# Input projections of both token mixers in seven block products, latents by way of DRAM, two dense down groups in one bank

## The chip, the cores and the metric

The kernel runs on one core of one Trainium2 chip. The metric is the device time of one execution in microseconds (us), taken as the median of several runs. Engines are named as in the profile: PE multiplies matrices, PEld loads its stationary operand, DVE (VectorE) and ACT (ScalarE) work element by element, POOL is GpSimd, and SP issues most transfers.

## What is computed

Two pre-norm residual layers on 1024 tokens of width 1024, then a final norm, all in float32. Each layer is a token mixer (latent attention and a gated recurrence side by side, fed by one input projection) and a channel mixer (a dense SwiGLU in layer 0, the top two of eight experts in layer 1).

```
for l in range(DEPTH):
    h = _rmsnorm(x, mix_norm[l])
    proj = h @ w_in[l]                          # 1024 x 1024 by 1024 x 2752
    c_q, c_kv, k_pe, hq, hf, hi, hg = jnp.split(proj, splits, axis=-1)
                                                # 384, 256, 64, then 4 x 512
    a = _mla(c_q, c_kv, k_pe, ...)              # latents normed, then w_q_b, w_kv_b, softmax
    r = _hgrn2(hq, hf, hi, hg, ...)             # 4 heads, chunkwise causal scan
    x = x + jnp.concatenate([a, r], axis=-1) @ w_out[l]
    h = _rmsnorm(x, ffn_norm[l])
    x = x + (_swiglu(h, ...) if l % 2 == 0 else _moe(h, ...))
return _rmsnorm(x, final_norm)
```

## The kernel before, in words

**Matmuls.** Every float32 operand of a matmul is split into a rounded high part (a copy on ACT, L162) and the rest (a subtraction on DVE, L163); `mm3` (L156 to L159) then multiplies high by high, high by low and low by high into the same bank. Most matmuls have 128 rows, 128 stationary columns and 512 moving columns.

**Input projection.** The norm of the eight token tiles (`norms`, `norm_tile`: square on ACT L184, power on POOL L181, multiplication on DVE L186) is followed tile by tile by eight transpositions on PE (L200) and a split of 128x1024 into the arena for split operands (FR). `Weights.parts` loads one block of 128 columns of w_in at a time (two raw buffers, SP) and splits it, again 128x1024. `proj` multiplies a block with the tokens: two halves of 512 tokens, eight steps in depth, three products, 48 matmuls. There are 22 blocks in a layer: three and two for the latents of queries and keys, one for the rotary key, then four for each of the four recurrence heads (forget gate, query, value, output gate). In layer 0 the first two blocks are done in pieces of 256 tokens, so that PE can start while later tiles arrive. Latents are squared on ACT from the bank, scaled on DVE (L354), summed on POOL (L353), and after the norm kept split in FR until attention uses them. Heads' values are evicted by ACT and DVE straight from the bank.

**Recurrence.** `hgrn` runs seven levels per head. A level copies a part of K (ACT, L455), multiplies four small products of 128 columns in two halves (PE, L487, eight matmuls), copies them under a mask into A (DVE, two operations, L494), and scales parts of Q and K by products of decays (DVE, four operations, L501). The next level's small products need those scaled parts. POOL makes the products of decays for the levels (L505). PE fills the time between levels with the projection of the next head, or, after the last head, with the first products of attention.

**Seven block products.** The dense gate and up projections already avoid one product in eight: operands are taken as 2 x 2 blocks, sums of blocks are formed, and seven products of blocks replace eight. `block_norms` makes the sums of the token operand (DVE and POOL) after the transpositions (L850), `block_sums` the sums of the weights (four POOL additions of 128x512, L879 to L884), `block_products` runs the seven products (L906, 12 matmuls of 512 columns each, 84 for a pair of column blocks) and combines them on eviction (four ACT copies, four DVE additions). For the first pair, `Gate.early` prepares three of the seven weight blocks, and their products run first over the first six token tiles (384 columns) and then over the last two (128 columns).

**Dense down.** Eleven groups of two blocks each; a group multiplies with all eight token tiles and DVE adds the bank to the residual x (`xt`). In the last group, a token tile's norm for layer 1 starts as soon as its two additions are done.

**Order.** A scheduler places the instructions; each engine then runs its own list in order, and waits where an operand isn't ready. Buffers are rings in two arenas, FF (float32) and FR (split operands).

## Time and profile before

| | |
|---|---|
| median of three runs | 3997.98 us (3994.89 to 4000.73) |
| profiled execution | 4001.75 us |
| its span, first to last instruction | 4000.0 us |
| mean granted clock of TensorE in it | 0.994 of full speed |
| PE busy | 3923.7 us (98%) |
| DVE, ACT, POOL busy | 2490.4, 1569.0, 353.5 us |

A row of a timeline gives start and duration in us, engine, line, operation, output and inputs with their shapes, the number of equal instructions in a row, and in brackets the idle time of the engine just before with what ended it. Rows of lines give a group's count, busy us and mean ns. Matmuls overlap each other, so the pace of PE is read from starts, not from durations.

The stages: layer 0's norm begins with the first transposition at 13 us, the small products of its recurrence heads start at 146, 210, 274 and 337 us, attention runs from about 371 to 531 us, then comes the output projection, the dense gate and up products from 622 to 1050 us, dense down to 1297 us; layer 1's mixer transposes its tokens from 1278 us on, and the experts run from 1933 us.

### The profile page before, as it was taken

The page shows a single profiled execution, that of the slowest core. Times are in us where ns is not written, and L with a number is a line of the kernel's source. Part 1 is how long each engine was busy: PE and PEld are TensorE (multiplying, and loading weights), DVE is VectorE, ACT ScalarE, POOL GpSimd, SP SyncE. Part 2 cuts the span into 40 slices and gives each one's busy share as a digit, 9 for nine tenths or more (in the row PEclk, how much of TensorE's full clock was granted, in tenths as well). Part 3 has the DMA queues.
Part 4 walks back from the last instruction along what each step waited for, and adds up shares of the span by engine and source line. Part 5 has one row for each costly group of instructions (what it writes and reads, how often), then busy time and mean ns, then how long its engine had stood idle before and what let it go on. Part 6 is the DMA issues. An engine that isn't in the chain of part 4 may idle for free. (4 is left out here: it accounts for less than half of the span.)

```text
span 4000.0 us, 62669 instructions
## 1 busy us (share of the span) xinstructions
PE 3923.7 (98%) x24870; PEld 3553.3 (89%) x24870; DVE 2490.4 (62%) x5624; ACT 1569.0 (39%) x2367; POOL 353.5 (9%) x406
## 2 busy tenths in 40 slices
PE   8999999999999999999899999999999999999998
PEld 7888887888788888888899999999999999999997
DVE  6455676554667454665655666776767765555665
ACT  3223434333312222442444334444444444444443
POOL 2100013233100101001200000000000000000011
PEclk9999999999999999999999999999999999999999
DMA  3111112222422111111665445455455555655674
GB/s 114 43 39 65 36 54 66 82 84 85 150 106 100 51 38 46 51 52 66 228 222 195 159 170 171 159 193 177 170 178 182 200 174 195 209 192 191 222 269 157
DMA packets 381228, 533.86 MB, mean 133 GB/s; under 512 B 15260, under 2 KB 317340, under 8 KB 380924
## 3 DMA queue, kind: packets, MB, share of 16 engines
q1 hardware_dynamic: 371142, 495.10, 37.1%
q0 software_dynamic: 7632, 26.95, 1.9%
q10 hardware_dynamic: 2150, 7.70, 0.5%
q8 instruction: 197, 3.23, 0.3%
q14 instruction: 107, 0.88, 0.1%
HBM read 478.82 MB, written 50.89 MB: 132 GB/s over the span
## 5 line engine op out<-in xcount | busy, mean ns | idle before, releaser
L157 PE MATMUL s<-fr_arena 128*128 128x256 f32 (+6 forms) x6816 | 2178.1, 320 | 11.1 <-ACT fr_arena L162 3.1
L158 PE MATMUL s<-fr_arena 128*128 128x256 f32 (+6 forms) x6816 | 2165.7, 318 | 0.0
L159 PE MATMUL s<-fr_arena 128*128 128x256 f32 (+6 forms) x6816 | 2162.7, 318 | 0.0
L157 PEld LDWEIGHTS s<-fr_arena 128*128 128x128 f32 x6816 | 1292.0, 190 | 94.0 <-ACT ff_arena L650 4.1
L159 PEld LDWEIGHTS s<-fr_arena 128*128 128x128 f32 x6816 | 1289.2, 189 | 75.2 <-DVE fr_arena L163 0.8
L158 PEld LDWEIGHTS s<-fr_arena 128*128 128x128 f32 x6816 | 1290.6, 189 | 71.5 <-DVE fr_arena L163 0.4
L1301 DVE TENSOR_TENSOR fr_arena<-ff_arena,fr_arena 128x256 fp32r<-128x256 f32 x2688 | 977.0, 418 | 552.6 <-ACT fr_arena L1298 548.2
L1298 ACT ACTIVATE fr_arena<-ff_arena 128x1024 fp32r<-128x1024 f32 x672 | 693.2, 1056 | 989.2 <-PE s L158 601.7
L162 ACT ACTIVATE fr_arena<-ff_arena 128x512 fp32r<-128x512 f32 (+7 forms) x598 | 354.8, 608 | 834.0 <-PE s L158 372.6
L163 DVE TENSOR_TENSOR fr_arena<-ff_arena,fr_arena 128x512 fp32r<-128x512 f32 (+8 forms) x598 | 419.6, 708 | 313.4 <-ACT fr_arena L162 244.3
L906 PE MATMUL s<-fr_arena 128*128 128x512 f32 (+2 forms) x1884 | 427.9, 389 | 0.7 <-ACT ff_arena L859 0.7
L906 PEld LDWEIGHTS s<-fr_arena 128*128 128x128 f32 x1884 | 350.3, 189 | 78.3 <-DVE ff_arena L924 4.1
L1408 DVE TENSOR_TENSOR ff_arena<-s,ff_arena 128x296 f32<-128x296 f32 (+3 forms) x416 | 176.2, 447 | 124.7 <-PE s L159 124.6
L1004 DVE TENSOR_TENSOR ff_arena<-s,ff_arena 128x512 f32<-128x512 f32 x176 | 119.1, 688 | 63.1 <-PE s L159 63.1
L162 ACT ACTIVATE fr_arena<-s 128x512 fp32r<-128x512 f32 (+7 forms) x182 | 109.8, 614 | 121.6 <-PE s L668 47.7
L1461 POOL DMA_DIRECT2D ff_arena<-xres x8 | 4.6, 576 | 1716.9 <-DMA ys<-ff_arena 1703.8
L163 DVE TENSOR_TENSOR fr_arena<-s,fr_arena 128x512 fp32r<-128x512 f32 (+7 forms) x182 | 126.6, 706 | 26.7 <-ACT fr_arena L162 24.6
L1362 DVE TENSOR_TENSOR ff_arena<-s,ff_arena 128x256 f32<-128x256 f32 (+4 forms) x224 | 95.8, 428 | 16.9 <-ACT ff_arena L1361 16.9
L1361 ACT ACTIVATE ff_arena<-s 128x256 f32<-128x256 f32 (+4 forms) x224 | 84.1, 376 | 23.0 <-PE s L159 23.0
L501 DVE TENSOR_TENSOR ff_arena<-ff_arena 128x256 f32<-128x256 f32 x224 | 84.5, 431 | 2.3 <-ACT ff_arena L455 1.5
L455 ACT ACTIVATE ff_arena<-ff_arena 128x256 f32<-128x256 f32 x112 | 42.8, 420 | 101.4 <-DVE ff_arena L501 42.5
L487 PEld LDWEIGHTS s<-ff_arena 128*128 128x128 f32 x448 | 55.4, 190 | 17.6 <-issue 14.2
(291 smaller groups left out, 1980.4 us busy)
## 6 DMA issues: line engine op xcount, KB each, us to landing
ff_arena<-in_moe_w_gate_dram SPq DMA_DIRECT2D x112, 1024.0 KB, 5.1
ff_arena<-in_moe_w_up_dram SPq DMA_DIRECT2D x112, 1024.0 KB, 7.5
ff_arena<-in_moe_w_down_dram SPq DMA_DIRECT2D x112, 1024.0 KB, 5.6
ff_arena<-in_w_in_dram SPq DMA_DIRECT2D x42, 512.0 KB, 4.0
ff_arena<-in_dense_w_gate_dram SPq DMA_DIRECT2D x11, 1024.0 KB, 5.8
ff_arena<-in_dense_w_up_dram SPq DMA_DIRECT2D x11, 1024.0 KB, 5.2
hidd<-ff_arena SPq DMA_DIRECT2D x44, 256.0 KB, 2.0
ff_arena<-hidd SPq DMA_DIRECT2D x11, 1024.0 KB, 6.6
```

The source lines that it names most:

```text
L157: nc.tensor.matmul(ps, lh, rh, start=first, stop=False)
L158: nc.tensor.matmul(ps, lh, rl, start=False, stop=False)
L159: nc.tensor.matmul(ps, ll, rh, start=False, stop=last)
L162: nc.scalar.activation(hi, src, AF.Copy)
L163: nc.vector.tensor_sub(lo, src, hi)
L501: nc.vector.tensor_mul(d, d, t)
L906: nc.tensor.matmul(ps, a[:, k, :], b[:, :, k, :], start=first and k + n == 0, stop=last and k == 3 and n == 2, skip_group_check=True)
L1004: nc.vector.tensor_add(xt[:, i, cs], ps, xt[:, i, cs])
L1298: nc.scalar.activation(hi, src, AF.Copy)
L1301: nc.vector.tensor_sub(lo[:, q:q + n], src[:, q:q + n], hi[:, q:q + n])
L1362: nc.vector.tensor_mul(s, ps[:, 1, 0:cap], s)
L1408: nc.vector.tensor_add(self.yT[:, k, :], ps[:, 0:cap], self.yT[:, k, :])
```

## The change

The mixers' input projections take the form of the dense gate's. `Weights` now holds eleven pairs of column blocks per layer: three for the latents with the rotary key, then two for each head (forget gate with query, value with output gate). `Weights.pair` forms the sums on POOL, splits seven weight blocks of 128x512 through a ring of twelve slots, runs the 84 matmuls, evicts by four ACT copies and four DVE additions into two float32 tiles of 1024, and loads the next pair into its only raw buffer. `early` prepares three blocks for the first pair as the gate does. The norm in front is `block_norms`; `norms`, `transpose_tile` and the pieces of 256 tokens are gone. What followed a bank before (sigmoids, squares, gains) now follows these tiles. The latents are normed in float32, written to a DRAM buffer `latd`, and read back and split by `attention`, whose first part runs before the last head's `hgrn` (`ahead`). The order of the seven products and of their evictions changes (for gate and up too). The last two dense down groups share one bank: 12 matmuls for each of the two banks of a token tile, 24 per tile, one DVE addition per bank in the place of two. Places in the arenas change throughout.

```
+            self.raw, self.s3 = view(FF, 4096, KD, 256), view(FF, 8192, 4, P)
+            self.wr = Ring(FR, 28672, 512, 12)
+            self.todo = [((0, 0, 256),), ((0, 256, 256),),
+                         ((0, 512, 192), (192, 672, 32), (224, 640, 32))]
+            self.todo += [((0, a, P), (P, b, P)) for a, b in hg]
...
+        def early(self):
+            self.load()
+            sums = block_sums(self.raw, self.s3)
+            self.ready = [block_parts(sums, self.wr) for _ in range(3)]
+            self.sums = iter([next(sums) for _ in range(4)])
+
+        def pair(self, d0, d1):
...
+            pa, pb = S2(), S2()
+            cs = [d.rearrange("p (q w t) -> p w q t", w=2, t=P)[:, w] for d in (d0, d1) for w in range(2)]
+            block_products(sums, self.wr, (pb[:, 0], pa[:, 0], pa[:, 1], pb[:, 1]), cs, ready)
+            if self.todo:
+                self.load()
...
+            for j in range((3, 2)[g]):
+                nc.sync.dma_start(latd[g * 3 + j], c32[g * 3 + j])
...
-        for u in range(2):
-            for b in range(2):
-                latent(b, u, first[b])
+        W.pair(c32[0], c32[1])
         if l == 0:
             setup_rope()
             setup_gates()
...
+        square(0)
+        square(1)
+        W.pair(c32[2], c32[3])
+        square(2)
+        square(3)
+        latent_rms(0)
...
         for h in range(H):
             f, K, Q, G, V = R["f"](T), R["k"](T), R["q"](T), R["g"](T), R["v"](NT, P)
-            ps = proj2(HC["f"] + h * P, rest if h == 0 else None)
-            nc.scalar.activation(f, ps, AF.Sigmoid)
-            nc.scalar.activation(K, ps, AF.Sigmoid, scale=-1.0)
+            W.pair(K, Q)
+            if h == 0:
+                rest()
+            nc.scalar.activation(f, K, AF.Sigmoid)
+            nc.scalar.activation(K, K, AF.Sigmoid, scale=-1.0)
...
+            if h == H - 1:
+                ahead()
             hgrn(h, f, K, Q, G, V, R)
...
+        for r, b, hl in raws[0:4]:
+            nc.sync.dma_start(r, latd[b])
         load_v(0)
         load_qk(0)
+        nc.sync.dma_start(tab, tabd)
+        for n, (r, b, hl) in enumerate(raws):
+            if n > 3:
+                nc.sync.dma_start(r, latd[b])
+            split(*hl, r)
+        yield
...
-    TN = ("B11", "B21", "T1", "T2", "B22", "T3", "T4")
+    TN = ("B21", "T1", "B11", "B22", "T2", "T4", "T3")
...
+        for i in range(NT):
+            for c in range(2):
+                cs = slice(c * 512, (c + 1) * 512)
+                ps = S1()
+                for b in range(4):
+                    mm3(ps, mv[i // 2][:, b, 0, i % 2], mv[i // 2][:, b, 1, i % 2], wv[:, b, 0, cs],
+                        wv[:, b, 1, cs], b == 0, b == 3)
+                nc.vector.tensor_add(xt[:, i, cs], ps, xt[:, i, cs])
+            post.tile(i)
```

Lines move: L162 and L163 become L174 and L175, the block transpositions L850 become L838, the block products L906 become L895 and their additions L906, the weights' sums L879 to L884 become L866 to L871, the recurrence's L494, L501 and L505 become L483, L490 and L494.

PE at the start of layer 0, before: transpositions of three tiles, then the projection in pieces of 256 tokens.

```order
L200 MATMUL s_126<-ident,ff_arena 128x128 x8
L200 MATMUL s_143<-ident,ff_arena 128x128 x8
L200 MATMUL s_161<-ident,ff_arena 128x128 x8
L157 MATMUL s_244<-fr_arena 128x256
L157 MATMUL s_295<-fr_arena 128x256
L158 MATMUL s_244<-fr_arena 128x256
L159 MATMUL s_244<-fr_arena 128x256
```

The same place after:

```order
L838 MATMUL s_126<-ident,ff_arena 128x128 x8
L838 MATMUL s_144<-ident,ff_arena 128x128 x8
L838 MATMUL s_184<-ident,ff_arena 128x128 x8
L838 MATMUL s_202<-ident,ff_arena 128x128 x8
L838 MATMUL s_231<-ident,ff_arena 128x128 x8
L838 MATMUL s_249<-ident,ff_arena 128x128 x8
L838 MATMUL s_273<-ident,ff_arena 128x128 x4
L838 MATMUL s_274<-ident,ff_arena 128x128 x4
L838 MATMUL s_287<-ident,ff_arena 128x128 x4
L838 MATMUL s_288<-ident,ff_arena 128x128 x4
L895 MATMUL s_312<-fr_arena 128x384 x24
L895 MATMUL s_313<-fr_arena 128x384 x12
```

The transpositions of all eight tiles now stand ahead of the first product, and that begins with 384 columns.

DVE in two levels of the recurrence, before (`s_2000`, `s_2014` and `s_2028` are the banks of the small products, masked copies L494, multiplications L501, a weight split L163):

```order
L494 COPY_PREDICATED ff_arena<-lmask,s_2000 128x4x16x4 x2
L501 TENSOR_TENSOR ff_arena<-ff_arena 128x4x16x4 x2
L501 TENSOR_TENSOR ff_arena<-ff_arena 128x4x4x16 x2
L494 COPY_PREDICATED ff_arena<-lmask,s_2014 128x4x8x8 x2
L501 TENSOR_TENSOR ff_arena<-ff_arena 128x4x8x8 x2
L501 TENSOR_TENSOR ff_arena<-ff_arena 128x4x2x32 x2
L163 TENSOR_TENSOR fr_arena<-ff_arena,fr_arena 128x1024
L494 COPY_PREDICATED ff_arena<-lmask,s_2028 128x4x4x16 x2
```

DVE in two levels after (masked copies L483, multiplications L490, L906 the eviction of a block product, L175 a weight split):

```order
L483 COPY_PREDICATED ff_arena<-lmask,s_2055 128x4x16x4 x2
L490 TENSOR_TENSOR ff_arena<-ff_arena 128x4x16x4 x2
L490 TENSOR_TENSOR ff_arena<-ff_arena 128x4x8x8 x2
L906 TENSOR_TENSOR ff_arena<-s_2201,ff_arena 128x4x128
L483 COPY_PREDICATED ff_arena<-lmask,s_2069 128x4x8x8 x2
L490 TENSOR_TENSOR ff_arena<-ff_arena 128x4x8x8 x2
L490 TENSOR_TENSOR ff_arena<-ff_arena 128x4x4x16 x2
L175 TENSOR_TENSOR fr_arena<-ff_arena,fr_arena 128x512
L483 COPY_PREDICATED ff_arena<-lmask,s_2083 128x4x4x16 x2
```

Before, a split of 1024 columns stood in every second level or so; now an operation of 512 columns stands in each.

POOL between two heads of layer 0, before (L505 the recurrence's products of decays, L181 a power for the read-out norm):

```order
L505 TENSOR_TENSOR ff_arena<-ff_arena 128x512
L505 TENSOR_TENSOR ff_arena<-ff_arena 128x256
L505 TENSOR_TENSOR ff_arena<-ff_arena 128x128
L505 TENSOR_TENSOR ff_arena<-ff_arena 128x64
L505 TENSOR_TENSOR ff_arena<-ff_arena 128x32
L505 TENSOR_TENSOR ff_arena<-ff_arena 128x16
L181 TENSOR_TENSOR rs_87<-rs_87,sm 128x4
L505 TENSOR_TENSOR ff_arena<-ff_arena 128x8
L181 TENSOR_TENSOR rs_87<-rs_87,sm 128x4
```

POOL between two heads after (L866 to L871 the sums of two pairs of weight blocks, L494 the products of decays):

```order
L866 TENSOR_TENSOR ff_arena<-ff_arena 128x512
L867 TENSOR_TENSOR ff_arena<-ff_arena 128x4x128
L870 TENSOR_TENSOR ff_arena<-ff_arena 128x4x128
L871 TENSOR_TENSOR ff_arena<-ff_arena 128x4x128
L866 TENSOR_TENSOR ff_arena<-ff_arena 128x512
L867 TENSOR_TENSOR ff_arena<-ff_arena 128x4x128
L870 TENSOR_TENSOR ff_arena<-ff_arena 128x4x128
L871 TENSOR_TENSOR ff_arena<-ff_arena 128x4x128
L494 TENSOR_TENSOR ff_arena<-ff_arena 128x512
L494 TENSOR_TENSOR ff_arena<-ff_arena 128x256
L494 TENSOR_TENSOR ff_arena<-ff_arena 128x128
```

Eight additions of 512 columns now stand ahead of a head's products of decays.

## Rows read from the trace of the kernel before

**Rows 1.** the profile page's first part: engine, busy us (share), matmuls.

```profile
PE 3923.7 (98%) x24870; PEld 3553.3 (89%) x24870; DVE 2490.4 (62%) x5624; ACT 1569.0 (39%) x2367; POOL 353.5 (9%) x406
```

**Rows 2.** stretches: length, busy us (instructions) of PE, PEld, DVE, ACT, POOL; clock; DMA.

```profile
200.00:260.00 60.00, 59.16 (x334) 49.65 (x334) 32.47 (x67) 15.69 (x28) 5.79 (x9) 1.00 0.16 44
...
700.00:800.00 100.00, 100.00 (x439) 81.74 (x438) 50.65 (x68) 39.87 (x68) 29.77 (x20) 1.00 0.25 82
...
1260.00:1300.00 40.00, 39.55 (x201) 32.81 (x200) 33.38 (x46) 18.00 (x25) 3.86 (x7) 1.00 0.37 132
```

**Rows 3.** PE's timeline in the recurrence: start, duration, engine, line, operation.

```profile
208.67 0.39 PE L159 MATMUL s<-fr_arena 128*128 128x512 f32 x1
...
210.26 0.94 PE L472 MATMUL s<-ff_arena 128*128 128x128 f32 x7
...
273.90 1.27 PE L472 MATMUL s<-ff_arena 128*128 128x128 f32 x10
```

**Rows 4.** PE's lines from 20.6 to 45 us: count, busy us, mean ns.

```profile
L157 PE MATMUL s<-fr_arena 128*128 128x256 f32 x49 | 14.6, 302 | 0.0
L158 PE MATMUL s<-fr_arena 128*128 128x256 f32 x49 | 14.3, 293 | 0.0
L159 PE MATMUL s<-fr_arena 128*128 128x256 f32 x48 | 14.2, 296 | 0.0
```

**Rows 5.** DVE's timeline at layer 0's start, and one row before the gate.

```profile
32.70 1.21 DVE L163 TENSOR_TENSOR fr_arena<-s,fr_arena 128x1024 fp32r<-128x1024 f32 x1
...
33.83 1.27 DVE L186 SCALAR_TENSOR_TENSOR ff_arena<-ff_arena,st 128x1024 f32<-128x1024 f32 x1
...
41.38 0.25 DVE L285 TENSOR_SCALAR lmask<-ff_arena 128x64 uint8<-128x64 f32 x1 [0.70 <-POOL ff_arena L283]
...
617.98 1.29 DVE L186 SCALAR_TENSOR_TENSOR ff_arena<-ff_arena,st 128x1024 f32<-128x1024 f32 x1 [0.66 <-POOL st L181]
```

**Rows 6.** PE's timeline at the start of the dense gate; idle time in brackets.

```profile
607.49 1.06 PE L850 MATMUL s<-ident,ff_arena 128*128 128x128 f32 x8 [0.97 <-DVE ff_arena L863]
...
619.32 1.97 PE L850 MATMUL s<-ident,ff_arena 128*128 128x128 f32 x8 [3.55 <-DVE ff_arena L186]
...
621.97 18.38 PE L906 MATMUL s<-fr_arena 128*128 128x384 f32 x99 [0.69 <-ACT ff_arena L859]
```

**Rows 7.** DVE's timeline over one level of the recurrence.

```profile
223.85 0.77 DVE L494 COPY_PREDICATED ff_arena<-lmask,s 128x256 f32<-128x256 uint8 x2 [0.64 <-PE s L487]
224.52 1.42 DVE L501 TENSOR_TENSOR ff_arena<-ff_arena 128x256 f32<-128x256 f32 x4
226.58 0.77 DVE L494 COPY_PREDICATED ff_arena<-lmask,s 128x256 f32<-128x256 uint8 x2 [0.64 <-PE s L487]
```

**Rows 8.** timelines of DVE, then of POOL, in the dense gate stage.

```profile
729.69 1.76 DVE L163 TENSOR_TENSOR fr_arena<-ff_arena,fr_arena 128x512 fp32r<-128x512 f32 x1
...
729.62 1.29 POOL L879 TENSOR_TENSOR ff_arena<-ff_arena 128x512 f32<-128x512 f32 x1 [12.87 <-DMA ff_arena<-in_dense_w_up_dram]
730.98 1.62 POOL L880 TENSOR_TENSOR ff_arena<-ff_arena 128x512 f32<-128x512 f32 x1
732.56 1.74 POOL L882 TENSOR_TENSOR ff_arena<-ff_arena 128x512 f32<-128x512 f32 x1
735.00 1.61 POOL L884 TENSOR_TENSOR ff_arena<-ff_arena 128x512 f32<-128x512 f32 x1 [0.69 <-DVE fr_arena L163]
```

**Rows 9.** DVE's lines, 140 to 400 us (two), then 625 to 1040 (two).

```profile
L501 DVE TENSOR_TENSOR ff_arena<-ff_arena 128x256 f32<-128x256 f32 x112 | 42.3, 431 | 1.2 <-ACT ff_arena L455 0.7
...
L163 DVE TENSOR_TENSOR fr_arena<-ff_arena,fr_arena 128x512 fp32r<-128x512 f32 x3 | 2.1, 686 | 0.8 <-PE s L159 0.8
...
L163 DVE TENSOR_TENSOR fr_arena<-ff_arena,fr_arena 128x512 fp32r<-128x512 f32 x148 | 127.6, 866 | 100.0 <-ACT fr_arena L162 98.6
L973 DVE TENSOR_TENSOR ff_arena<-ff_arena 128x512 f32<-128x512 f32 x41 | 38.1, 949 | 0.0
```

**Rows 10.** POOL's lines, 0 to 140 us.

```profile
L353 POOL TENSOR_TENSOR ff_arena<-ff_arena 128x512 f32<-128x512 f32 x6 | 8.8, 1461 | 20.2 <-ACT ff_arena L352 20.2
```

332 lines of the change are left out of this document (149 added, 183 removed).

## The prediction

> **What bounds the kernel now.** I read the busy shares first. TensorE is busy for 3923.7 of 4000.0 us [rows 1], so what shortens the kernel must take matmuls away, and what lengthens it must open a gap on TensorE. The table by stretches says where a gap could open [rows 2]. In the recurrence (200 to 260 us) PE is busy for 59.16 of 60 us and DVE for 32.47; in the dense gate and up products (700 to 800 us), which already have the form that the mixers now take, PE is busy for 100.00 of 100 and DVE for 50.65, with POOL at 29.77; at the start of layer 1's mixer (1260 to 1300 us) PE has 39.55 of 40. So TensorE ends last in all three, and DVE has room on average. Whether it has room at each place is read from single levels of the recurrence [rows 7]. All sums below are differences, made against the profiled execution (4001.75 us, of which the span is 4000.0) and then applied to the median, 3997.98, which is 3.8 lower.
>
> **Part 1: matmuls removed.** Before, a layer's 22 column blocks take 22 x 48 = 1056 matmuls of 512 columns; after, 11 pairs take 7 x 12 = 84 each, 924. The order of the changed kernel bears the counts out. One costs 0.227 us: seven starts between 208.67 and 210.26 [rows 3]. So 239.7 us become 209.7: 30.0 less per layer, 60.0 in all, if PE stays fed. The two dense down groups that now share a bank keep their number of matmuls; 16 adds on DVE go, on an engine that nobody waits for there (33.38 of 40 us busy [rows 2]): nothing.
>
> **Part 2: layer 0 starts later.** Before, PE projects while the tokens still arrive: 49 + 49 + 48 = 146 matmuls of 256 columns are issued by 45 us [rows 4], worth 73 of 512 columns, 16.6 us. Left at 45 us: 239.7 - 16.6 = 223.1. After, every transposition stands ahead of the first product. That product's start: the last norm multiplication was at 33.83 [rows 5]. Ahead of it now stand 21 DVE operations of 512 columns in the place of 9 of 1024. The long ones follow each other by 1.13 (32.70 to 33.83 [rows 5]), the short ones last 0.69 [rows 9], and less the same overlap of 0.08 advance by 0.61: 12.8 against 10.2, so 2.6. Seven small mask operations with their casts come ahead of it too, about 0.25 each, so 2. The first pair's four sums on POOL and the operand residues run beside it; half of the 4.3 that a set costs at most (part 4) is 2. From the last norm multiplication to the first product the dense gate took 617.98 to 621.97, 4.0 [rows 5, 6]. Sum 33.8 + 2.6 + 2 + 2 + 4.0 = 44.4, taken as 45. Bounds: 38, if only the 4.0 counts; 50, if a whole set counts (4.3) and each of the seven masks waits 0.70 for POOL, as one does at 41.38 [rows 5] (33.8 + 2.6 + 4.3 + 4.9 + 4.0 = 49.6). What remains then is 209.7 plus the cost of beginning in slices of 384 and 128 columns on a clock not yet full: the dense gate's first 99 matmuls, 63 whole ones by area, took 18.38 us [rows 6] where 63 x 0.227 = 14.3, so 4.1. Gain of layer 0: 223.1 - 213.8 = 9.3; 17 for 38, 4 for 50.
>
> **Part 3: layer 1 starts like the dense gate.** The merged down groups give 24 matmuls for each token tile, then come the transpositions and the sliced products, as at the gate before. There PE idled 0.97 + 3.55 + 0.69 = 5.2 and its last eight transpositions took 1.97 in place of 1.06 [rows 6]: 6.1, with the 4.1 of slices 10.2. The old start lost 40 - 39.55 = 0.45 [rows 2]. Gain: 30.0 - 10.2 + 0.4 = 20.2. I give it 2 either way, since nothing in it is foreign to the gate.
>
> **Part 4: POOL's sums beside the recurrence.** One level of the recurrence is a ring: two predicated copies and four multiplications on DVE (223.85 to the end of 224.52 + 1.42, about 2.1 us), then eight small matmuls on PE, for which DVE waits 0.64; a level takes 2.73, 223.85 to 226.58 [rows 7], and eight or so projection matmuls cover it on PE. After, the weight split or the eviction of a product puts one more DVE operation of about 0.6 in each level: 2.1 + 0.6 = 2.7 of 2.73. It fits, with nothing to spare. Into this now fall four POOL sums of 512 columns per head, six times (three heads in each layer whose levels run under the next head's projection). What a sum does to DVE: alone, a split's subtraction takes 686 ns and a recurrence multiplication 431 [rows 9]; a subtraction that ran beside a sum took 1.76 [rows 8], 1.08 more, so 4.3 for a set of four if every sum hits such an operation. Over the whole gate stage the same subtraction averages 866 ns (148 of them) and the multiplication of gate and up 949 (41), against 686: (148 x 0.18 + 41 x 0.26) / 21 sets = 1.8 per set [rows 9]. I take 1.8, because that row holds 21 sets of the very same sums beside the very same splits, while 4.3 rests on one pile-up. 6 x 1.8 = 10.8. Bounds: 0, if DVE catches up in the levels with more matmuls above them, and 6 x 4.3 = 26.
>
> **Part 5: latents.** The latents go to DRAM and are read back and split while the last head's recurrence runs; the loads have some 79 matmuls (18 us) above them. The root mean squares now hang on a copy out of the bank, a square on ACT and a POOL addition of 1024 columns, two of 1.46 [rows 10], so about 2.9, under 16 products of 3.6 us. On SP's queue a latent's write waits for its multiplication, and the load of the next pair, now with one raw buffer, stands behind the write; the six blocks already split (72 matmuls, 16.3 us) cover that, as they do in the dense gate with its one buffer (100.00 of 100 [rows 2]): nothing, or a few us per layer if the cover is gone. I have no row for the splits queued in order on ACT and DVE behind a load. I take 5 for both layers, nearer to the lower end, since each step by itself is covered; the ends are 0 and 16 (each layer's reload exposed by 5 and each root mean square by 1.5).
>
> **Sum.** 9.3 + 20.2 - 10.8 - 5 = 13.7 us gained: 3997.98 - 13.7 = 3984.
>
> **Rivals.**
> *The sums cost nothing.* Only the late starts and some of the latents count: 9.3 + 20.2, less 0 to 5, gives 3968 to 3973. For it: DVE's average share, and PE's 100.00 of 100 in the dense stage with four sums per pair [rows 2]. Against it: in that stage no ring passes from DVE to PE and back.
> *Every sum stretches one DVE operation by 1.08.* 9.3 + 20.2 - 26 - 5 = -1.5: 3999, no change. For it: the pile-up of [rows 8] is what a set looks like when DVE has no pause, and 2.7 of 2.73 is no pause. The same time comes from a start of layer 0 at 50 with the latents at 16: 4 + 20.2 - 10.8 - 16 = -2.6, 4001.
> *Slower: each sum stops the recurrence for its whole length.* The multiplications read two operands in SBUF, as the subtraction beside the sum did; that one began at 729.69 and was over at 731.45, 0.54 after the sum's end at 730.91 [rows 8], so it looks less slowed than held back. Where every operation of the ring depends on the one before, nothing is made up between the sums: 1.29 + 1.62 + 1.74 + 1.61 = 6.26 per set [rows 8], 37.6 for six, and 9.3 + 20.2 - 37.6 - 5 = -13.1: 4011. It decides against the change from 24.5 / 6 = 4.1 per set on, and shows as slower from 5.4 on. Against it: POOL pauses between sums for the splits, and the ring's predicated copies read a bank.
> The Trainium skill speaks for this rival: "SBUF — State Buffer", section "Who interferes with whom", says that a VectorE instruction with two SBUF inputs contends with a GpSimd instruction that reads SBUF, under an exclusive lock in which the loser waits for the whole instruction. By that rule the sum would be the one of this rival, 4011; by the mean over the stage it is 3984. The trace agrees for the pile-up (1.76 for 0.69) and not for the mean (866 for 686 ns).
>
> **How the numbers follow.** A run of this kernel can tell about 0.2%, 8 us, from no change. Chances: the forecast 0.43 (its own range, 3975 to 3994, straddles 3990: 0.33 of it faster, 0.10 same); sums free 0.21, all faster; one stretch per sum 0.20 (0.01 faster, 0.17 same, 0.02 slower); whole stops 0.16 (0.02 same, 0.14 slower). Faster 0.55, same 0.29, slower 0.16. The range leaves out most of the last case, and above the others goes to 4004; below it reaches the free sums with the better half of layer 0's bound (38 to 45): 3964.
>
> **What would show it.** Right: PE's first product of layer 0 near 45 us and a gap of about 5 us ahead of layer 1's first; heads 58 to 61 us apart where they were 63.64 (210.26 to 273.90 [rows 3]; 63.64 - 24 x 0.227 = 58.2 is the floor); the muls of a recurrence level above 431 ns beside POOL. Wrong: heads still 63 us or more apart (whole stops), or a mean of the level's multiplications that hasn't moved (free sums); a first product after 50 us; a gap of over 8 us between the last recurrence and attention.

## The result, and the profile after

The change makes the kernel slower: median 4054.32 us (4049.52 to 4057.07, four runs) against 3996.43 (3994.67 to 4000.73, four runs), ratio 1.0141 [1.0126, 1.0157]. The forecast was 3984, with a range up to 4004. The profiled execution has a span of 4053.3 us, 53.3 more than before, and its mean granted clock is 0.985 where it was 0.994.

The page's first part, engine, busy us (share) and instructions:

```profile
PE 3908.6 (96%) x24582; PEld 3520.4 (87%) x24582; DVE 2601.2 (64%) x5844; ACT 1669.7 (41%) x2603; POOL 492.9 (12%) x512
```

Beside [rows 1], PE has 288 instructions fewer. By area that is the 264 matmuls of 512 columns that were counted; the rest is how the first blocks are cut (192 of 256 columns in layer 0 before; 36 of 384 and 36 of 128 in each layer after). But PE lost only 15.1 us of busy time, a quarter of the 60 that the 264 are worth, and it stands still for 68 us more. POOL's 139 us more are the new sums, squares and residues. Where the time went is told by four marks that both kernels have: the last small product of a head's first level (L472 before, L461 after), the dense gate's first product, and layer 1's last transposition. Each column is later (+) or earlier (-) than the kernel before over that stretch, in us; the last two columns are experiments that come below.

| stretch | before, length | forecast | after | e13: POOL's new work on DVE | e16: the best version |
|---|---|---|---|---|---|
| start to layer 0's first head | 148.3 | +7.0 | +34.6 | +17.5 | +13.9 |
| three head periods, layer 0 | 191.0 | -10.9 | +1.7 | -10.9 | -15.1 |
| last head, attention, to the gate | 282.7 | +2.5 | +0.4 | +1.0 | -0.1 |
| gate to layer 1's last transposition | 682.2 | 0 | 0.0 | -0.1 | +1.0 |
| from there to layer 1's first head | 114.3 | -3.9 | +17.0 | +9.3 | +2.0 |
| three head periods, layer 1 | 190.9 | -10.9 | +1.4 | -10.7 | -14.7 |
| last head to the end | 2390.6 | +2.5 | -1.8 | -1.6 | -0.6 |
| span | 4000.0 | -13.7 | +53.3 | +4.5 | -13.6 |

(The forecast's column divides its own gains: 24 matmuls fewer per head at 0.227 are 5.4, less 1.8 for the sums, three periods per layer; what remains of its 9.3 and 20.2 lies ahead of the first heads; its 5 for the latents stand in halves behind the last heads.) So the loss has two places of about the same size: the heads didn't become shorter, 25 us behind the forecast, and both mixers take far longer to reach their first head, 48 us behind it.

**The heads.** PE's timeline, twice the same small products, one head apart (start, duration):

```profile
238.68 0.83 PE L461 MATMUL s<-ff_arena 128*128 128x128 f32 x6
...
302.69 0.83 PE L461 MATMUL s<-ff_arena 128*128 128x128 f32 x6
```

They are 64.01 apart where [rows 3] has 63.64 with 24 matmuls more. The levels between, first on DVE's timeline:

```profile
256.40 1.46 DVE L490 TENSOR_TENSOR ff_arena<-ff_arena 128x256 f32<-128x256 f32 x4
...
258.50 0.78 DVE L483 COPY_PREDICATED ff_arena<-lmask,s 128x256 f32<-128x256 uint8 x2
259.17 2.81 DVE L490 TENSOR_TENSOR ff_arena<-ff_arena 128x256 f32<-128x256 f32 x4
...
268.78 3.09 DVE L490 TENSOR_TENSOR ff_arena<-ff_arena 128x256 f32<-128x256 f32 x4
```

Then on POOL's:

```profile
258.29 1.33 POOL L866 TENSOR_TENSOR ff_arena<-ff_arena 128x512 f32<-128x512 f32 x1 [18.20 <-DMA ff_arena<-in_w_in_dram]
259.69 1.33 POOL L867 TENSOR_TENSOR ff_arena<-ff_arena 128x512 f32<-128x512 f32 x1
268.23 1.29 POOL L870 TENSOR_TENSOR ff_arena<-ff_arena 128x512 f32<-128x512 f32 x1 [7.20 <-DVE fr_arena L175]
269.60 1.32 POOL L871 TENSOR_TENSOR ff_arena<-ff_arena 128x512 f32<-128x512 f32 x1
```

And on PE's, idle time in brackets:

```profile
261.46 1.13 PE L476 MATMUL s<-ff_arena 128*128 128x128 f32 x8 [1.15 <-DVE ff_arena L490]
...
271.35 1.13 PE L476 MATMUL s<-ff_arena 128*128 128x128 f32 x8 [1.46 <-DVE ff_arena L490]
```

A level's four multiplications take 1.46 alone ([rows 7] has 1.42) and 2.81 and 3.09 beside a pair of POOL's sums, 1.35 and 1.63 more; the predicated copies under the first sum took their usual 0.78. How the time is lost is seen in single multiplications. The first two of those at 259.17, on DVE's timeline one by one:

```profile
259.17 0.72 DVE L490 TENSOR_TENSOR ff_arena<-ff_arena 128x256 f32<-128x256 f32 x1
259.82 1.49 DVE L490 TENSOR_TENSOR ff_arena<-ff_arena 128x256 f32<-128x256 f32 x1
```

Alone, one takes 0.42. Each of these began while a sum ran and ended 0.27 and 0.29 after that sum (259.62 and 261.02). The same holds for all 24 that began beside a sum in this trace, four in each of six heads: however much of the sum was left, from 0.44 to 1.21 us, they ended 0.28 after it, to within 0.01. So a sum holds back a multiplication that begins beside it until the sum is over, and the four add up to 3.0 us a head (0.30, 1.07, 0.60 and 1.06 in this one). The eight projection matmuls that cover such a level on PE don't reach, and PE waits 1.15 and 1.46.

**The starts.** Stretches of the span: length, busy us (instructions) of PE, PEld, DVE, ACT, POOL; granted clock; DMA:

```profile
20.00:60.00 40.00, 18.63 (x83) 17.18 (x84) 34.94 (x61) 22.18 (x40) 25.00 (x61) 0.60 0.13 40
100.00:200.00 100.00, 94.19 (x420) 74.54 (x419) 52.83 (x91) 37.41 (x66) 34.90 (x29) 0.93 0.24 74
...
1340.00:1480.00 140.00, 129.94 (x577) 104.86 (x576) 64.53 (x104) 53.62 (x90) 49.14 (x38) 0.92 0.21 66
```

At the very start DVE is busy 34.94 of 40 us and PE 18.63: here the norm's chain, on DVE with ACT and POOL, ends last. Behind the first product, which starts at 52.53, PE is fed for 94.19 of 100 and 129.94 of 140 us at a clock of 0.93 and 0.92. What PE waits for, summed over the span (waiting line, releaser: us, times, longest):

```profile
PE s L476 <- DVE ff_arena L490: 16.2, 12, 1.7
PE s L895 <- ACT ff_arena L903: 12.1, 14, 1.9
PE s L537 <- POOL rs L191: 11.1, 16, 0.8
PE s L357 <- POOL ff_arena L350: 7.3, 4, 3.2
```

The first row is the levels. The second is evictions by ACT: the next product's bank comes free late. The last is the latents' sum of squares, which POOL adds. What such a gap does is seen in layer 1, PE's timeline with idle time in brackets:

```profile
1388.98 2.61 PE L357 MATMUL s<-sm,ff_arena 128*128 128x1 f32 x16 [3.23 <-POOL ff_arena L350]
1391.45 7.36 PE L895 MATMUL s<-fr_arena 128*128 128x512 f32 x20
```

After 3.23 us of idling and sixteen matmuls of one column each, twenty products take 7.20 by their starts (the next instruction begins at 1398.65) where 20 x 0.227 = 4.5: the gap costs its own length and then 2.7 more. The stretch 1380 to 1400 has a granted clock of 0.83, so part of it ran at the lower of the two levels (1.2 GHz).

### The profile page after: what moved, and what is told of

The parts are those of the page before. It is cut to its first block, busy times and chain, and to the rows that moved or that the text cites. A ratio compares the mean times of both kernels' runs of the same rounds, so it can differ in the third digit from the quotient of the medians.

```text
span 4053.3 us, 62819 instructions
## 1 busy us (share of the span) xinstructions
PE 3908.6 (96%) x24582; PEld 3520.4 (87%) x24582; DVE 2601.2 (64%) x5844; ACT 1669.7 (41%) x2603; POOL 492.9 (12%) x512
## 5 line engine op out<-in xcount | busy, mean ns | idle before, releaser
L169 PE MATMUL s<-fr_arena 128*128 128x256 f32 (+6 forms) x6080 | 1893.5, 312 | 8.8 <-ACT fr_arena L1316 2.5
L170 PE MATMUL s<-fr_arena 128*128 128x256 f32 (+6 forms) x6080 | 1884.2, 310 | 0.0
L171 PE MATMUL s<-fr_arena 128*128 128x256 f32 (+6 forms) x6080 | 1881.3, 310 | 0.0
L169 PEld LDWEIGHTS s<-fr_arena 128*128 128x128 f32 x6080 | 1153.5, 190 | 67.6 <-ACT ff_arena L638 3.7
L171 PEld LDWEIGHTS s<-fr_arena 128*128 128x128 f32 x6080 | 1151.0, 189 | 50.3 <-DVE fr_arena L175 0.7
L170 PEld LDWEIGHTS s<-fr_arena 128*128 128x128 f32 x6080 | 1152.2, 190 | 47.2
L895 PE MATMUL s<-fr_arena 128*128 128x512 f32 (+2 forms) x3804 | 912.7, 396 | 18.2 <-ACT ff_arena L903 12.1
L895 PEld LDWEIGHTS s<-fr_arena 128*128 128x128 f32 x3804 | 705.5, 192 | 179.3 <-ACT ff_arena L903 27.7
L174 ACT ACTIVATE fr_arena<-ff_arena 128x512 fp32r<-128x512 f32 (+8 forms) x708 | 404.9, 586 | 852.5 <-PE s L895 261.0
L175 DVE TENSOR_TENSOR fr_arena<-ff_arena,fr_arena 128x512 fp32r<-128x512 f32 (+8 forms) x708 | 457.3, 653 | 247.7 <-ACT fr_arena L174 240.0
L906 DVE TENSOR_TENSOR ff_arena<-s,ff_arena 128x512 f32<-128x512 f32 x176 | 117.2, 687 | 162.4 <-PE s L895 156.4
L866 POOL TENSOR_TENSOR ff_arena<-ff_arena 128x512 f32<-128x512 f32 x44 | 62.2, 1414 | 765.2 <-DMA ff_arena<-in_dense_w_gate_dram 314.4
L174 ACT ACTIVATE fr_arena<-s 128x512 fp32r<-128x512 f32 (+4 forms) x186 | 105.2, 575 | 94.4 <-PE s L656 40.7
L175 DVE TENSOR_TENSOR fr_arena<-s,fr_arena 128x512 fp32r<-128x512 f32 (+4 forms) x186 | 121.1, 661 | 22.3 <-ACT fr_arena L174 20.3
L1002 DVE TENSOR_TENSOR ff_arena<-s,ff_arena 128x512 f32<-128x512 f32 x144 | 97.3, 688 | 49.0 <-PE s L171 48.9
L903 ACT ACTIVATE ff_arena<-s 128x512 f32<-128x512 f32 x176 | 102.1, 580 | 15.3 <-PE s L895 12.9
L490 DVE TENSOR_TENSOR ff_arena<-ff_arena 128x256 f32<-128x256 f32 x224 | 99.8, 503 | 0.0
```

Source lines behind the costliest of these rows:

```text
L169: nc.tensor.matmul(ps, lh, rh, start=first, stop=False)
L170: nc.tensor.matmul(ps, lh, rl, start=False, stop=False)
L171: nc.tensor.matmul(ps, ll, rh, start=False, stop=last)
L174: nc.scalar.activation(hi, src, AF.Copy)
L175: nc.vector.tensor_sub(lo, src, hi)
L490: nc.vector.tensor_mul(d, d, t)
```

## The experiments

Each time below is that of one run, where no count is given, beside runs of the kernel before at 3995 to 3997. Runs of one and the same kernel spread by several us (after: 4049.5 to 4057.1), so a difference of a few us between two single times is left open, and marks inside the traces decide. Those have a spread too: e4, which leaves layer 0 as it is, reached its first head at 179.9 where after has 182.9. The lines of all kernels are those of after, but for e6.

### Whose fault are the sums: e1, e2, e7

**e1** multiplies raw blocks where the sums of weight blocks would stand; the four sums on POOL are left out in the mixers.

```
- sums = block_sums(self.raw, self.s3)
+ sums = block_plain(self.raw)      # yields seven raw blocks
```

> The changed kernel with the four POOL sums of each pair left out in both mixers: the weight splits read the raw blocks themselves, so the mixers' projections are not computed. Number of matmuls, splits, evictions and loads is that of the changed kernel. Theory POOL: the sums stall the multiplications of the recurrence (in the changed kernel two of seven levels took 2.8 and 3.1 us on DVE where 1.43 is usual) and hold the splits of the latents' pairs back. Then heads come 61.1 us apart in place of 64.0, the first head of layer 0 some 5 us earlier, and the whole is about 4025 to 4032 us. Rival RING: DVE's extra operation in each level fills the ring by itself. Then heads stay 63.5 us or more apart and the whole stays above 4045 us.

Measured: 4100.8, but that time can't be compared. The mixers' values are others, so other tokens go to the experts, and the stretch behind the mixers changes. Up to there the trace can be read: heads 61.0 apart, the first product at 47.8, the first head reached at 171.3 in place of 182.9, layer 1's last head 39.7 earlier than in after. Theory POOL's period for the heads held, 3.0 less than in after, which is what DVE loses a head; the first head gained 11.6 where it gave 5. That the whole would show it was a mistake in the design, so the next two keep the values.

**e2** forms the same sums on DVE. **e7** puts one of the four back on POOL.

```
- nc.gpsimd.tensor_sub(s3, a11, a21)       # and three more
+ nc.vector.tensor_sub(s3, a11, a21)       # e7: this one on nc.gpsimd again
```

> The changed kernel with the mixers' sums on DVE in place of POOL (0.6 us each, 8 per head; nothing left out). Theory POOL: the stall of 2.9 us per head is gone, the added DVE work costs part of it back; heads 61.5 to 63 us apart, the whole 4035 to 4048 us. Rival RING: 2.4 to 4.8 us more DVE work per head goes straight into the ring; heads 65 us or more apart, the whole 4060 us or more.

> The changed kernel with three of the four sums on DVE as in run e2 (4016, heads 59.5 us apart) and one, which the seventh product alone needs, on POOL. It tells contention from the wait in the chain of sums and splits: nothing waits for this sum soon. Theory CONTENTION: each POOL sum stops a multiplication of the recurrence for about its own length of 1.3 us when it falls in a level. Then heads come 60.2 to 60.9 us apart and the whole is 4020 to 4025 us. Rival CHAIN: the POOL sums hurt because splits wait for them; with one that is needed late the heads stay 59.3 to 59.8 us apart and the whole 4013 to 4018 us.

e2: 4016.1, 38 us less than after. Two of its heads, on PE's timeline:

```profile
224.53 0.83 PE L461 MATMUL s<-ff_arena 128*128 128x128 f32 x6
...
283.93 0.83 PE L461 MATMUL s<-ff_arena 128*128 128x128 f32 x6
```

59.40 apart: the four sums, 0.69 each on DVE, cost less there than as neighbours. Heads and whole came out better than either theory gave. They are also closer together than e1's, which forms no sums at all, so the stall isn't all that e2 gains. PE's waits in one period, the second of layer 0, part it (us):

| | period | at the levels, for DVE (L476 <- L490) | in the read-out norm, for POOL (L537 <- L191) | for a bank, for ACT (L895 <- L903) |
|---|---|---|---|---|
| after | 64.0 | 2.6 | 1.5 | 0.7 |
| e1 | 61.0 | 0 | 1.5 | 0.8 |
| e7 | 60.8 | 0 | 1.0 | 0.8 |
| e2 | 59.4 | 0 | 0.5 | 0 |

From after to e1 the stall goes. From e1 to e2 two other waits shrink; POOL's sums don't cause them, since e1 has none, and why they shrink no run shows. e7: 4030.8. Its one sum, on POOL's timeline:

```profile
246.47 1.29 POOL L866 TENSOR_TENSOR ff_arena<-ff_arena 128x512 f32<-128x512 f32 x1 [23.82 <-DMA ff_arena<-in_w_in_dram]
```

The multiplications beside it, on DVE's, and those of the next level:

```profile
247.31 1.73 DVE L490 TENSOR_TENSOR ff_arena<-ff_arena 128x256 f32<-128x256 f32 x4
...
250.36 1.42 DVE L490 TENSOR_TENSOR ff_arena<-ff_arena 128x256 f32<-128x256 f32 x4
```

The sum ends at 247.76; the first multiplication, which began 0.45 before that, ended 0.28 after it, and the four take 0.31 longer. All six that began beside a sum in e7 did the same. Yet PE has no wait at a level here (table above): the first two periods of each layer are 1.3 to 1.6 longer than e2's by the two other waits, and the third is not (60.9 for 60.9, 60.9 for 62.5). So neither theory holds as written. The sum stops a multiplication, but for 0.3 and not 1.3, and that doesn't reach PE; the periods came near CONTENTION's range for another reason. All four sums on POOL made six periods 24.3 longer than e2's, 4.1 each, and 20.1 longer than e1's. The mean of that multiplication over 190 to 340 us, from DVE's lines by shape (count, busy us, mean ns), in after:

```profile
L490 DVE TENSOR_TENSOR ff_arena<-ff_arena 128x256 f32<-128x256 f32 x80 | 38.5, 539 | 0.0
```

In e2:

```profile
L490 DVE TENSOR_TENSOR ff_arena<-ff_arena 128x256 f32<-128x256 f32 x67 | 24.2, 419 | 0.0
```

That is [rows 9]'s 431 raised by a quarter, and back. e7's whole is 14.7 over e2's, but 6.2 of that lie behind the last head, where both are the same; up to there it lost 8.6.

### The start and layer 1: e3, e4

**e3** asks whether a low clock at the start makes the first head late: transpositions of data already there, whose results nobody reads, keep PE at work between the token tiles. **e4** undoes the merged down groups alone.

```
+ for k in range(n[i]):                     # e3, n = 0, 50, 0, 70, 0, 10, 16, 10
+     nc.tensor.transpose(wt[:, 0:P], h[:, k % 4 * P:(k % 4 + 1) * P], ident)
- for g in (NGD - 2, NGD - 1):              # e4: the last group by itself again
+ for g in (NGD - 1,):
```

> The changed kernel with idle transpositions (50 after token tile 1, 70 after tile 3, 10, 16 and 10 after tiles 5 to 7) put into TensorE's gaps of layer 0's norm; their results are not used. Theory CLOCK: the first products of layer 0 run at half clock because TensorE sat idle in 13 to 50 us (granted clock 0.59 to 0.61 in 20 to 60 us, 0.91 in 60 to 80). With the gaps filled the first product stands where it stood, 52 to 53 us, the first 99 matmuls of the block products take about 15 us in place of 21, and the whole is 4 to 7 us shorter, 4047 to 4051 us. Rival LATE: only the late start counts; the whole stays within 2 us of the changed kernel's 4054.

> The changed kernel with the last two dense down groups apart again: ten groups as before the change, and the last group alone in the new layout, 12 matmuls per token tile in place of 24 above the norm of layer 1. If the merge is worth what the form of the gate's start suggests, TensorE's idle time ahead of layer 1's first product grows from 6.0 us to 15 or more and the whole goes to 4063 us or more. If the merge is worth nothing (DVE and not the cover sets the pace of that norm), the whole stays at 4050 to 4058 us.

e3: 4060.4. In its first stretch (columns as for after):

```profile
20.00:60.00 40.00, 30.78 (x211) 29.36 (x209) 36.22 (x64) 22.45 (x40) 25.52 (x63) 0.87 0.13 41
```

The clock rose from 0.60 to 0.87, and the first head came at 180.0, 2.9 earlier than in after and no earlier than in e4, which has no fillers. Neither theory holds as written, since the whole got no shorter and no term of 6 us more was foreseen; a fuller clock at the start is worth at most 3 us of the 34.6, perhaps nothing. What PE waits for there is not its own.

e4: 4063.1, 9 more than after. PE's timeline ahead of layer 1's first product, idle time in brackets:

```profile
1328.03 1.06 PE L838 MATMUL s<-ident,ff_arena 128*128 128x128 f32 x8 [2.60 <-DVE ff_arena L851]
...
1339.72 3.60 PE L838 MATMUL s<-ident,ff_arena 128*128 128x128 f32 x16 [5.16 <-DVE ff_arena L851]
1345.62 1.09 PE L838 MATMUL s<-ident,ff_arena 128*128 128x128 f32 x8 [2.30 <-DVE ff_arena L196]
1348.22 1.97 PE L838 MATMUL s<-ident,ff_arena 128*128 128x128 f32 x8 [1.52 <-DVE ff_arena L196]
1351.90 2.58 PE L895 MATMUL s<-fr_arena 128*128 128x384 f32 x7 [1.71 <-ACT fr_arena L174]
```

That is 13.3 us of idling. The same places in after:

```profile
1313.87 1.06 PE L838 MATMUL s<-ident,ff_arena 128*128 128x128 f32 x8 [0.50 <-POOL fr_arena L856]
...
1327.58 1.06 PE L838 MATMUL s<-ident,ff_arena 128*128 128x128 f32 x8 [0.85 <-DVE ff_arena L851]
...
1339.40 1.97 PE L838 MATMUL s<-ident,ff_arena 128*128 128x128 f32 x8 [3.52 <-DVE ff_arena L196]
1342.48 9.82 PE L895 MATMUL s<-fr_arena 128*128 128x384 f32 x53 [1.11 <-ACT fr_arena L174]
```

Those are 6.0. The merged groups give DVE the time for the norm's chain; they are worth about 9 us, and the loss is elsewhere.

### Order and place around the first products: e5, e6, e8, e9

All four build on e2. **e5** moves the one product that needs no sum (T4 with a22) and its eviction ahead of B22. **e6** starts layer 0's first products on the first four token tiles, after tile 6, in two halves of 256 columns. **e8** makes layer 0's gate masks one pair later. **e9** (on e5) exchanges the places of value and output gate, so that an eviction no longer lands where a latent is still being written to DRAM.

```
+ product(b4, "T4", True, True); copy(c21, b4)       # e5, ahead of product(b3, "B22", ...)
+ if l == 0 and i == 6: W.begin()                    # e6
- W.pair(c32[0], c32[1]); setup_gates()              # e8: behind the second pair
+ W.pair(c32[2], c32[3]); setup_gates()
- ("g", T, (12800, 13824)), ("v", T, (14848, 15872)) # e9, with what follows from it
+ ("g", T, (13824, 12800)), ("v", T, (15872, 14848))
```

> The changed kernel with the sums on DVE (run e2: 4016) and with the product T4, which has a bank of its own, moved from sixth to fourth of the seven, so that each of the two banks that collect several products has two products of time for its eviction where it had one. Theory EVICTION: TensorE's 10.4 us of waits for ACT's copies out of a bank (10 of them, in both mixers) come from that single product of slack, and some are followed by products at half clock. Then those waits fall below 4 us and the whole comes to 4002 to 4010 us. Rival QUEUE: ACT is late because its own list holds splits and sigmoids ahead of the copy, and a product more of slack doesn't help: waits of 8 us or more, the whole 4013 us or more.

> The changed kernel with the sums on DVE (run e2: 4016), and layer 0's first three products cut into two halves of 256 columns: the first half runs as soon as the first four token tiles are done, between the transpositions of the later tiles, in place of 384 columns behind all transpositions. Theory LATE START: layer 0 loses because TensorE has nothing to multiply before 49.5 us. Then the first product starts near 40 us, 36 of 108 quarter-width shares are done by 50 us, and the first head of layer 0 comes 5 to 9 us earlier; the whole 4007 to 4011 us. Rival CHAIN: what follows is paced by DVE and by the chain of loads, sums, splits and evictions; the first head comes at most 2 us earlier and the whole stays at 4014 us or more.

> The changed kernel with the sums on DVE (run e2: 4016), and the set-up of masks and gates issued one pair of products later in the program, so that fewer of the 14 mask operations with POOL's counters stand on DVE ahead of layer 0's first product. Theory LATE START: the first product comes 1 to 3 us earlier than 49.5 and the whole is shorter by as much, 4013 to 4015 us. Rival: DVE's norm work alone sets the start, and first product and whole move by less than 1 us.

> The kernel of run e5 (4014.6) with the two places of the recurrence's value and gate tiles in the other order, so that the first head's evictions don't land where the last latents still wait to be written to DRAM. In e5 ACT's copy out of a bank waited 1.24 us for the write of a latent, and TensorE 2.66 and 2.64 us in the two layers (157 and 1423 us). Theory PLACE: this detour by DRAM costs those waits and some products at half clock behind them: both gaps fall under 1 us, the first heads come 2 to 4 us earlier each, the whole 4007 to 4011 us. Rival QUEUE: ACT's own list (sigmoids, a table load, splits) holds the copy as long; the gaps stay above 2 us and the whole at 4013 us or more.

e5: 4014.6, 1.5 less than e2, within the spread. PE's waits for ACT's copies fell from 10.4 to 7.0, between its theory and its rival, while those for DVE's evictions rose from 2.7 to 5.7. Five of the six periods became shorter (58.2 to 59.0, the sixth stayed at 62.4), and the first head came 3.5 later. Layer 1's worst gap in it, on PE's timeline:

```profile
1425.87 12.51 PE L895 MATMUL s<-fr_arena 128*128 128x512 f32 x48 [2.64 <-ACT ff_arena L903]
```

The eviction that ends it, on ACT's timeline:

```profile
1425.21 0.60 ACT L903 ACTIVATE ff_arena<-s 128x512 f32<-128x512 f32 x1 [1.24 <-DMA latd<-ff_arena]
```

ACT, working its list in order, stood 1.24 for a latent's write to DRAM, and PE behind it. In e9 this gap and its twin in layer 0 are 0.30 and the time is 4008.6, 6 less: the place was the cause of the two waits. What it is worth is less sure. Layer 1's first head came 4.1 earlier behind the last transposition and its third period is 3.3 shorter; layer 0's first head, which the theory had 2 to 4 earlier, came 0.4 later.

e6: 4024.2, 8 more than e2. PE's timeline in it (its L853 and L910 are L838 and L895 of the others):

```profile
36.28 7.15 PE L910 MATMUL s<-fr_arena 128*128 128x256 f32 x36 [1.71 <-ACT fr_arena L174]
...
55.07 2.02 PE L910 MATMUL s<-fr_arena 128*128 128x256 f32 x11 [3.46 <-DVE fr_arena L871]
```

PE's first product came at 36.28, 13 earlier than in e2, then PE waited for the token operand again, and the first head came 5.6 later. What decides is the chain that makes the operand's parts; cutting PE's work finer only moves the wait. That was the rival.

e8: 4014.9, the first product at 49.6 as in e2 (49.5). But this doesn't clear the masks. DVE's line for the mask comparisons up to the first product, in e2 and then in e8:

```profile
L280 DVE TENSOR_SCALAR lmask<-ff_arena 128x64 uint8<-128x64 f32 x4 | 1.9, 466 | 1.8 <-POOL ff_arena L278 1.8
...
L280 DVE TENSOR_SCALAR lmask<-ff_arena 128x64 uint8<-128x64 f32 x4 | 1.9, 464 | 1.8 <-POOL ff_arena L278 1.8
```

The scheduler put the same four ahead of it in both, so the edit changed nothing there and its question stays open.

### All that helped, and more: e10, e11, e12, e15, e16

**e10** is e9 with e8's order and with the squares of the latents added on DVE. **e11** (on e10) prepares the first weights after token tile 5 instead of 3. **e12** (on e10) puts the residues of layer 0's token sums on DVE. **e15** (on e12) makes the masks after the third pair.

```
- nc.gpsimd.tensor_add(sacc[g], sacc[g], sq)                      # e10
+ nc.vector.tensor_add(sacc[g], sacc[g], sq)
- if l == 0 and i == 3:                                           # e11
+ if l == 0 and i == 5:
- (nc.vector if i == NT - 1 else nc.gpsimd).tensor_sub(lo, t, hi) # e12: lo_eng is DVE for l == 0
+ (nc.vector if i == NT - 1 else lo_eng).tensor_sub(lo, t, hi)
```

> The kernel of run e9 with masks and gates set up one pair later (run e8's edit) and the latents' sum of squares on DVE in place of POOL (1.2 us in place of 2.9). Theory CHAIN: TensorE's waits ahead of the root mean squares (0.6 to 1.7 us, four of them) and those at 63 and 87 us on DVE's eviction go, with the products at half clock behind them: 3 to 7 us below e9. Rival: other steps of the same chains are as late; within 2 us of e9.

> The kernel of run e10 with the first pair's weights (load, sums, three splits) issued after token tile 5 in place of tile 3. Theory DVE: layer 0's norm is paced by DVE, whose list holds 7 weight operations (4.3 us) ahead of the third tile; moved, they fill DVE's own waits, the first product comes 2 to 4 us earlier than 49.5, and the whole is 2 to 4 us below e10. Rival: the first product then waits for the weights; no gain, or up to 3 us of loss.

> The kernel of run e10 with the twelve residues of layer 0's token sums (1.26 us each on POOL) on DVE, 0.6 us each. Theory CONTENTION: beside POOL's residues DVE's norm multiplications took 2.28 in place of 1.28 us and splits 1.38; without them the start gets back about as much as the added 7.2 us of DVE work costs or more, and the first product comes 0 to 3 us earlier. Rival DVE: only the added work counts; the first product comes 4 to 7 us later and the whole is longer by as much.

> The kernel of run e12 (3989) with masks and gates set up after the third pair and their scratch at another place. TensorE waited 1.91 us at 58 us for an eviction that stood behind mask operations on DVE, and seven products at half clock followed. If the masks now stand behind it, 2 to 4 us shorter, 3985 to 3987 us; if the scheduler puts them ahead again, no change.

e10: 3990.4, 18 less than e9, where its theory gave 3 to 7. Of that the first head takes 9.7 (167.6 after 177.3) and layer 1's 3.9 (116.5 behind the last transposition, after 120.4); 4.0 lie behind the last head, where nothing was edited, and so belong to the spread. e11: 3995.1, 4.7 more than e10, of which 4.2 lie behind the last head, with the first product hardly earlier (48.5 after 49.3): its theory falls. e12: 3988.9; the whole moved within the spread, but the first product came 5.5 earlier, at 43.7, and the first head 5.2. That is more than its theory gave, and the residues are not all that moved: in e10 ten of the 28 mask operations (comparisons, shifts, casts) stand on DVE ahead of the first product, in e12 one. e15: 3987.5, 1.4 less than e12: open.

**e16** is e12 once more, in 11 runs.

> The kernel of run e12, word for word, timed in five rounds beside the kernel before. By the single run (3988.9 beside 3995.7) it is 0.1 to 0.25% shorter than the kernel before; if that was the scatter of one run, the interval reaches 1.

3988.09 median (3986.90 to 3992.56, 11 runs) against 3996.59 (3994.27 to 4000.46, 15 runs): ratio 0.9979 [0.9970, 0.9988]. It is 0.2% faster than the kernel before, and the interval leaves out 1. Its page's first part:

```profile
PE 3887.1 (98%) x24582; PEld 3507.6 (88%) x24582; DVE 2646.7 (66%) x5950; ACT 1673.5 (42%) x2603; POOL 342.7 (9%) x406
```

The same stretches as for after:

```profile
20.00:60.00 40.00, 24.18 (x125) 21.87 (x125) 37.99 (x72) 23.51 (x43) 4.40 (x44) 0.88 0.13 40
100.00:200.00 100.00, 98.86 (x512) 80.47 (x511) 76.95 (x145) 43.06 (x76) 13.17 (x18) 1.00 0.24 74
...
1340.00:1480.00 140.00, 138.30 (x702) 112.68 (x703) 98.93 (x177) 59.69 (x104) 15.33 (x20) 1.00 0.23 68
```

DVE does more (76.95 for 52.83, 98.93 for 64.53) and PE waits less: 98.86 of 100 and 138.30 of 140, at the full level.

### The two causes apart: e13, e14

**e13** is after with nothing but POOL's new work moved to DVE (sums, squares, layer 0's residues); order and places are those of after. **e14** leaves that work on POOL and has the three edits of order and place (T4 fourth, masks later, places exchanged).

> The changed kernel with nothing but POOL's element work of the mixers moved to DVE: the sums of the weights (run e2's edit), the latents' sums of squares, and layer 0's twelve residues; product order, places and masks as in the changed kernel. Theory POOL: nearly all of the 58 us lost, and of the 65 us won back by run e12 (3989), is POOL's work beside and ahead of DVE. Then the whole is 3990 to 4000 us. Rival CHAINS: product order, places and masks carry a share of their own that doesn't shrink with POOL's; then it is 4003 to 4012 us.

> The changed kernel with POOL's work left where it is and the other edits alone: product T4 fourth (run e5), the places of value and gate tiles in the other order (run e9), masks and gates set up one pair later (run e8). Theory POOL: with the sums on POOL the chains are held elsewhere and these edits are worth little: 4046 to 4054 us. Rival CHAINS: they are worth what they were worth with the sums on DVE and more, 4035 to 4044 us.

e13: 4006.3, 48 less than after. e14: 4041.1, 13 less. Together 61 of the 66 us between after and e16. Both rivals hold: order and places carry a share of their own. Two stretches of e13:

```profile
20.00:60.00 40.00, 26.25 (x129) 23.89 (x130) 38.45 (x74) 23.89 (x43) 4.62 (x45) 0.68 0.12 40
100.00:200.00 100.00, 96.54 (x487) 77.81 (x487) 74.60 (x134) 41.80 (x75) 11.74 (x16) 1.00 0.22 69
```

By the table above, POOL's work costs 12.6 and 12.1 in the two layers' heads (4.1 a head) and 17.1 and 7.7 ahead of the first heads: half of it is where the prediction put 2 us (part 2) or thought it covered (part 5). The cost is that of the move, with what the scheduler changes for it: in e13, as in e12, one mask operation stands ahead of the first product, in after sixteen. e14's first head came at 179.7, 14 after e13's, and its heads stayed 63.0 to 64.6 apart.

## Why the prediction was wrong

**Right.** Matmuls and their pace (part 1): 264 fewer by area, 0.227 each; the floor of 58.2 a head, which e16 comes near with 58.6. Layer 1's idling ahead of its first product (part 3's 5.2): 0.50 + 0.85 + 3.52 + 1.11 = 6.0. Latents read back under the last head's recurrence (part 5): the stretch to the gate grew by 0.4.

**Wrong, part 4: the size of a sum.** I took 1.8 us per set, because that row held "21 sets of the very same sums beside the very same splits" [rows 9]. That mean is what DVE loses in a stage with slack. It says nothing of a ring in which the four multiplications stand between one level and the next and no engine can go ahead. There the stall is 3.0 a head, by DVE's own rows and by e1; with the sums moved to DVE six periods are 24.3 (e2) and 24.7 (e13) shorter, 4.1 each, where the forecast has 10.8 in all. The bound of 26 held, the value did not. The sums aren't the whole miss in the heads. After's six periods are 35.8 above the floor of 58.2: 24.7 of it goes with POOL's work (e13), 8 more with order and places (e16), for which the forecast had no term, and 3 remain.

The rival *whole stops* had the mechanism: a sum holds the multiplication beside it to its own end, in 24 cases of 24. Its 6.26 a set was too dear, since only the part of a sum that is left when a multiplication begins counts; beside it predicated copies and evictions of a bank go on (in the heads 17 and 11 that began under a sum took their usual 0.43 and 0.69). It put the point from which it decides at 4.1, just what the move of the sums gave; with the other terms as forecast the change would have come out about neutral. The Trainium skill's rule ("SBUF — State Buffer", section "Who interferes with whom"), by which DVE's work with two inputs in SBUF and POOL's reads exclude each other, agrees with these rows, and not with the mean over the stage, on which I chose to rely.

**Wrong, part 2: what stands ahead of the first product, and behind it.** The first product was put at 45 with 50 as its bound; it came at 52.53. Three things were missing or too small. The first: POOL's sums and residues hold DVE's operations here too, eight of them for 6.4 us in all ahead of the first product, where the sum has 2. DVE's timeline in after shows the same multiplication twice, the second beside sums on POOL (the fence behind it):

```profile
13.71 1.29 DVE L196 SCALAR_TENSOR_TENSOR ff_arena<-ff_arena,st 128x1024 f32<-128x1024 f32 x1
15.45 2.28 DVE L196 SCALAR_TENSOR_TENSOR ff_arena<-ff_arena,st 128x1024 f32<-128x1024 f32 x1 [0.45 <-POOL st L191]
```

POOL's timeline at that place:

```profile
15.38 1.26 POOL L866 TENSOR_TENSOR ff_arena<-ff_arena 128x512 f32<-128x512 f32 x1
16.72 2.13 POOL L867 TENSOR_TENSOR ff_arena<-ff_arena 128x512 f32<-128x512 f32 x1
```

The second: the seven mask comparisons with their shifts and casts took 5.0 in place of 2; 1.9 of that is the lengthening of two comparisons beside residues, counted in the 6.4. The third is a place in the arena. The square for the last token tile is written where POOL still reads for its residues, so ACT waits for POOL and DVE for ACT. ACT's timeline, then DVE's:

```profile
45.51 1.06 ACT L194 ACTIVATE ff_arena<-ff_arena 128x1024 f32<-128x1024 f32 x1 [3.39 <-POOL fr_arena L856]
...
46.69 0.15 DVE L189 TENSOR_SCALAR st<-st 128x1 f32<-128x1 f32 x1 [1.69 <-ACT ff_arena L194]
```

In e12 and e13, with the residues on DVE, the first product comes at 43.7 and 44.0: no operation of DVE is held ahead of it, ACT doesn't wait for POOL, and one mask operation is left there. That these agree with the forecast's 45 is luck, since nine more operations of 512 columns stand on DVE ahead of it than in after. What each of the three is worth by itself no run shows.

And the step "What remains then is 209.7 plus the cost of beginning in slices" took PE as fed from the first product on. It isn't. The first head was 27.6 later than forecast, of which the first product is 7.5; behind it PE idled for 8.5 us up to the first head, and its matmuls ran below the full clock (0.93 from 100 to 200).

**Wrong, part 3: "nothing in it is foreign to the gate".** It was given 2 either way, and layer 1's first head came 20.9 later than forecast. The start is the gate's, but what follows is not: latents are squared on ACT and POOL, normed, written to DRAM, and the evictions of five pairs stand in the same in-order lists of ACT and DVE. In layer 1 that stretch lost 5.0 to the squares on POOL (3.23 and 1.77), 2.7 to evictions behind other work on ACT, and more to the lower clock after each gap (0.92 over 140 us). The experiments part it: POOL's work 7.7, order and place 7.3 (e13 to e16), and 5.9 that even e16 misses against the forecast.

**Wrong, part 5: a cover that wasn't one.** POOL's addition for the root mean squares was put at 2.9 under 3.6 us of products. PE waited 7.3 us for it, four times: the addition had begun late, behind the copy and the square on ACT. With the conflict of places (some 6 by e9) that is 13, inside the bounds of 0 to 16. For a queue behind a load I had no row; what came was an eviction behind a write, because of a place in an arena. And the comparison "as they do in the dense gate with its one buffer" was false: gate and up alternate between two raw buffers, the mixers have one.

**The sum.** 13.7 forecast as gain, 53.3 measured as loss, 67 apart: 25 in the heads (part 4, and order and places), 28 and 21 ahead of the first heads (parts 2, 3, 5), and 6 less lost behind them. The forecast's own case, a kernel in which the seven products gain, exists, though at 8.5 and not 13.7: it is e16, once POOL's work is off DVE's way.

**What stays open.** 14 us of layer 0's start remain in e16: the 146 matmuls of [rows 4] ran while tokens arrived, and e6's way of cutting the new ones finer didn't bring that back. Whether e15's 1.4 is real, and how much of after's 182.9 is spread (e4 has 179.9), these runs don't tell; nor why the two waits that e1 shares with after shrink in e2.

## What to carry to other kernels

Work given to POOL "because it is idle" is only free beside DVE work that can slip. Ask of every POOL operation on SBUF which DVE operations run beside it, and whether those stand in a ring or in a chain that ends last; then price it by what is left of the POOL operation when DVE's begins, not by the stage's mean. And when PE's work is shortened, price the stretch between its first product and the first steady loop as a stage of its own: list the evictions and splits in the order of each engine's list, and count every gap twice, once for itself and once for the slower matmuls behind it.
